# FFN-down with ten instead of nine of sixteen squares in seven-product form, the residual kept off chip between sweeps, and some weight sums moved into w_out

## The chip, the core and the metric

The kernel runs on one NeuronCore of a Trainium2 chip. TensorE (PE) multiplies, VectorE (DVE) and ScalarE (ACT) do the elementwise work, SyncE (SP) issues nearly all DMAs, in order, on one queue. The metric is the device time of one execution in microseconds (us).

## The reference

One decoder layer on 256 tokens of width 2048, in float32. Only the middle matters here:

```
x  = x + mix @ w_out                                   # 2048 x 2048
h2 = rms_norm(x, mlp_norm)
x  = x + square(relu(h2 @ w_ffn_up)) @ w_ffn_down      # 2048 x 8192, 8192 x 2048
gate = sigmoid(rms_norm(x, ple_norm) @ w_ple_gate)
x  = x + gate * (p @ w_ple_proj)
out = rms_norm(x, final_norm)
```

Ahead of it stand an input projection, a pooling mixer and an RWKV-7 time mixer, which the change does not touch.

## The kernel before, in words

Every matrix product is made from rounded parts: an operand a is split in a high part (a rounded copy, made by ScalarE) and a low part (a minus its high part, made by VectorE), and a product is three matmuls: high by high, low by high, high by low. So each weight that comes from DRAM passes through ScalarE and VectorE before PE can use it.

*Buffers.* Weights land in `raw` buffers, a ring of six [128, 1024] tiles (`RING`, L151; three in one pool, three in a later pool), and are split into rings of five `wh` (high) and four `wl` (low). A load waits on SP until its buffer is free, and what stands behind it on SP waits too. Big fixed buffers `a0` to `a5` ([128, 2048] each, `a8`) hold activations and the residual x, which is two tiles of 1 MiB, one for output columns 0 to 1023 (pair 0) and one for 1024 to 2047 (pair 1).

*w_out* (`gemm_toks`, from L1170): four chunks of 512 output columns, each of eight double rows of weights, 96 matmuls a chunk. After each chunk the new part of x is transposed into `h2`.

*FFN-up* (`gemm_wide`, L1121; matmuls L1135 and L1140) runs in two halves (`ffn_half`) of eight chunks f; each chunk has two groups of 16 k rows, and after each group `square` (L1410 to L1412) takes relu and square out of the wide PSUM bank. Each group gives one "pair" of activation rows, 16 per half. The chunks of the second half are f = 8 to 15.

*FFN-down* follows each half as two sweeps (`sweep`), one for each pair of output columns, with 16 "squares" each: a 2 by 2 block product of activations (two k tiles, two token tiles) by weights b11, b12, b21, b22 (two k tiles, two groups of 512 columns). A *plain* square makes the eight block products, 24 matmuls of 512 columns. A *seven-product* square uses a Strassen-like form: seven products, 21 matmuls. Three of them (p1, p2, p3) use the blocks b11, b21, b22 ("of_blocks"), four (p5, p7, p6, p4) use sums of blocks t1 to t4 ("of_sums"). p2, p3, p4 and d22 are PSUM banks shared with the plain squares; p1, p6, p5, p7 lie in two wide banks w1 and w2, and are combined by VectorE (the tile u, L1362 to L1365) after the last seven-product square. All matmuls of a sweep are recorded at one line, L1230; the tile in its name is d_p (banks p2, p3, p4), d_d (d22) or d_w (wide banks).

*Weights of a seven-product square* (`weights_seven`): w7h and w7l are the high and low parts of the blocks (L1281 to L1284), the four sums are made in place in the raw buffers (L1286 to L1289), and th and tl are their high and low parts (L1292, L1294). th and tl have one buffer each. For the squares in `AHEAD` the sums are made earlier, during FFN-up, by `sums_ahead` (VectorE L1219, L1223, L1224 from raw_ta into ta), stored to DRAM (L1226, tile tad) and loaded again in the sweep into buffer a4 (L1339, tile tr). One `sums_ahead` follows each FFN-up chunk. Before: `PLAIN` is 0, 3, 6, 9, 12, 14, 15, `AHEAD` is 2, 5, 8, 11, and the other seven-product squares are 1, 4, 7, 10, 13.

*Order in a seven-product square.* If the next square is also of seven products, the sums come first, else the blocks, so that th and tl of the next one can be written early. PE's order was written by hand only up to w_out; from there the scheduler orders every engine's instructions by priorities and its own estimate of when they are ready, and that order is fixed when the kernel is built.

*Residual.* x for the two pairs lies in buffers a3 and a4. The result of a sweep is scaled and added to it (`scaled_residual`, L1384): two wide ones after u, and four of 512 columns at the end of the last square. `x_store` (L1388) and `x_load` (L1391) move a tile of x to DRAM and back: pair 1 goes out after chunk 1, and at square 3 of the second sweep of each half the x of the other pair goes out and the one of this sweep comes into a3. In the last sweep pair 1 comes into a4 at square 12, with the load of p (`split_p`).

Of the kernel before, what the change touches and what calls it, by code (L numbers as in the profile page):

```python
# [40 lines left out]
def trunk(  # L41
# [62 lines left out]
    make_identity(nc, ident)  # L104
    ones = const.tile([128, 128], F32, name="ones")
    with tc.high_priority(40000):
# [1038 lines left out]
    def transposed(name):  # L1145
# [22 lines left out]
        return part, lambda k: hl[:, :, k, :]  # L1168

    h2_part, h2 = transposed("h2")  # L1170
# [33 lines left out]

    PLAIN = (0, 3, 6, 9, 12, 14, 15)
    AHEAD = (2, 5, 8, 11)
    SEVEN = tuple(i for i in range(16) if i not in PLAIN)
    dr = ctx.enter_context(tc.tile_pool(name="dr", bufs=1, space=bass.MemoryType.DRAM))
    saved = {}

    def sums_ahead(hf, np_, i):

        ra, rb = (
            load_raw(w_down[np_, hf * 16 + i, r].rearrange("p a n -> p (a n)"), 1024, f"ta{hf}{np_}_{i}_{r}") for r in range(2)
        )
        b11, b22, b12, b21 = ra[:, 0:512], ra[:, 512:1024], rb[:, 0:512], rb[:, 512:1024]
        t = fp.tile([128, 4, 512], F32, tag="th", name=f"ta{hf}{np_}_{i}")
        with tc.high_priority(20000):
            nc.vector.tensor_tensor(  # L1219
                t[:, 1:3], ra.rearrange("p (c n) -> p c n", c=2)[:, ::-1], b12.unsqueeze(1).to_broadcast([128, 2, 512]),  # L1220
                op=ALU.subtract,
            )
            nc.vector.tensor_tensor(t[:, 0], b11, t[:, 1], op=ALU.add)  # L1223
            nc.vector.tensor_tensor(t[:, 3], b21, t[:, 0], op=ALU.subtract)  # L1224
        d_ = saved[hf, np_, i] = dr.tile([128, 2, 1024], F32, tag=f"ta{hf}{np_}_{i}", name=f"tad{hf}{np_}_{i}")
        nc.sync.dma_start(d_.rearrange("p r n -> p (r n)"), t.rearrange("p c n -> p (c n)"))  # L1226
    F_A11, F_A12, F_A22, F_S2, F_S3, F_S4, F_S1 = range(7)
# [12 lines left out]
    def square_plain(src, pr):  # L1240

        q = PLAIN.index(pr)
        if pr == PLAIN[-1]:
            plains[:] = [fp.tile([128, 1024], F32R, tag="yd", name=f"yd{pr}")]
        elif q % 2 == 0:
            plains[:] = [a8((1, 2, 0)[q // 2], f"yd{pr}", F32R)]
        d = plains[0][:, q % 2 * 1024 : (q % 2 + 1) * 1024]
        split_sb(d[:, 0:512], d[:, 512:1024], src)

        def block(i, j):  # L1250
            o = j * T + i * 128
            return d[:, o : o + 128], d[:, 512 + o : 512 + o + 128]

        return block

    def square_seven(src, pr):

        if pr == SEVEN[-1]:
            y = a8(5, f"ys{pr}", F32R)[:, 0:1792]
        else:  # L1260
            y = fp.tile([128, 1792], F32R, tag="ys", bufs=NYS, name=f"ys{pr}")
# [41 lines left out]

    def sweep(src, acts, hf, np_, name, residual_, hooks=()):
# [22 lines left out]
        for i in range(npair):  # L1327
# [4 lines left out]
            if kept_sums is None:  # L1332
                rb, tr = load_raw(src[np_, i, 1].rearrange("p a n -> p (a n)"), 1024, f"{name}_1_{i}"), None
            else:
                rb = ring("raw", F32, f"raw_{name}_1_{i}")
                nc.sync.dma_start(rb[:, 512:1024], src[np_, i, 1, :, 1])
                tr = a8(4, f"tr_{name}_{i}").rearrange("p (r n) -> p r n", r=2)
                for r in range(2):
                    nc.sync.dma_start(tr[:, r], kept_sums[:, r])  # L1339
                tr = [tr[:, r] for r in range(2)]  # L1340
            if i in SEVEN:
# [44 lines left out]
    def x_store(np_):  # L1386
        xd[np_] = dr.tile([128, 2, 1024], F32, tag=f"xd{len(xd)}{np_}", name=f"xd{len(xd)}{np_}")
        nc.sync.dma_start(xd[np_], xc.pop(np_))  # L1388
# [4 lines left out]
    def split_p():  # L1393
# [4 lines left out]
        return t_[:, 0:512], t_[:, 512:1024]  # L1398

    xd, ps_ = {}, []  # L1400

    def ffn_half(hf):
        acts = []
        for i in range(8):
# [189 lines left out]
```

## Time and profile before

| | before |
|---|---|
| median of 3 runs | 1166.19 us (1165.98 to 1168.64) |
| profiled execution | 1166.29 us |
| its span, first to last instruction | 1164.2 us |
| busy: PE, VectorE, ScalarE | 1153.3, 903.5, 686.2 us |
| granted TensorE clock, mean | 0.999 |
| w_out chunks 1 to 3 with the transposes | about 303 to 371 us of the span |
| FFN-up half 0, then sweeps 1 and 2 | about 371 to 551, 551 to 632, 632 to 713 us |
| FFN-up half 1, then sweeps 3 and 4 | about 713 to 891, 891 to 972, 972 to 1053 us |
| DMA traffic | 269.36 MB |

How to read it: busy time is the time in which an engine has an instruction in work. PE's matmuls overlap and their ends are modelled, so PE's busy time also covers short waits; what a matmul costs is read from the distance of starts. The chain of waits is followed back from the last instruction: each piece was either released by the piece before it or came next on its engine. In a row with a bracket, the bracket gives the idle time of the engine just before the instruction and what ended it.

### The profile page before, as it was taken

The numbers are of one execution on the slowest core, as the hardware profiler recorded it, in microseconds if no ns is written. First come the engines' busy times: TensorE is split into PE (matmuls) and PEld (weight loads), VectorE is DVE, ScalarE is ACT, GpSimd is POOL, SyncE is SP. The second block draws the span as 40 slices with busy tenths as digits, with TensorE's granted clock in tenths as the row PEclk, the third lists the DMA queues.
The fourth block names the chain that finished last, engine by engine and source line by source line (L and its number), as shares of the span: only waits on it lengthen the run. The fifth ranks groups of instructions, "written<-read, shape, count | busy, mean of one in ns | idle before, by whom it ended". The sixth has DMA issues, their size and how long they took to land.

```text
span 1164.2 us, 19240 instructions
## 1 busy us (share of the span) xinstructions
PE 1153.3 (99%) x7360; PEld 991.6 (85%) x7360; DVE 903.5 (78%) x1193; ACT 686.2 (59%) x1216; POOL 17.2 (1%) x77
## 2 busy tenths in 40 slices
PE   9999999999999999999999999999999999999997
PEld 8999998788888888888888888888888888888886
DVE  7886898356555887887989988778878899898843
ACT  5868555667555555555665664555555664669733
POOL 4100000000000000000000000000000000000000
PEclk9999999999999999999999999999999999999999
DMA  7554444453766888787776867878987777876812
GB/s 274 164 172 129 157 155 148 146 164 109 254 190 212 298 313 285 257 305 263 250 265 236 300 234 240 313 273 286 320 291 234 265 270 260 289 285 223 301 55 73
DMA packets 73547, 269.36 MB, mean 231 GB/s; under 512 B 8176, under 2 KB 9200, under 8 KB 70512
## 3 DMA queue, kind: packets, MB, share of 16 engines
q1 hardware_dynamic: 73168, 267.78, 66.9%
q8 instruction: 57, 0.93, 0.3%
q10 hardware_dynamic: 288, 0.37, 0.1%
q14 instruction: 34, 0.28, 0.1%
HBM read 246.09 MB, written 22.02 MB: 230 GB/s over the span
## 4 chain that ended last, share of the span: by engine, by line
PE 97%; DVE 1%; ACT 1%; DMA 0%; issue 0%; ACTq 0%; DVEq 0%
PE u_w L1135 20%; PE d_p L1230 16%; PE u_w L1140 10%; PE d_w L1230 8%; PE d_d L1230 3%; PE o_b L193 2%; PE o_b L194 2%; PE o_b L195 2%; PE gt_b L193 2%; PE gt_b L195 2%; PE gt_b L194 2%; PE zp_b L193 1%; PE wag_b L380 1%; PE zr_b L184 1%; PE zk_b L184 1%; PE zk_b L185 1%
## 5 line engine op out<-in xcount | busy, mean ns | idle before, releaser
L1135 PE MATMUL u_w<-h,wh_u 128*128 128x512 f32 x1024 | 321.7, 395 | 0.0
L171 ACT ACTIVATE wh_u<-raw_u 128x512 fp32r<-128x512 f32 x256 | 147.5, 624 | 155.9 <-PE u_w L1135 107.7
L1140 PEld LDWEIGHTS u_w<-h,wl_u 128*128 128x128 f32 x1024 | 192.3, 188 | 45.3
L1140 PE MATMUL u_w<-h,wl_u 128*128 128x256 f32 x1024 | 201.5, 278 | 0.0
L172 DVE TENSOR_TENSOR wl_u<-raw_u,wh_u 128x1024 fp32r<-128x1024 f32 x128 | 156.2, 1221 | 47.3 <-PE u_w L1140 36.3
L1135 PEld LDWEIGHTS u_w<-h,wh_u 128*128 128x128 f32 x1024 | 156.0, 189 | 0.1
L1230 PE MATMUL d_p<-wh_d,yd 128*128 128x512 f32 x336 | 89.8, 389 | 0.0
L1230 PEld LDWEIGHTS d_p<-wh_d,yd 128*128 128x128 f32 x336 | 62.9, 188 | 13.0
L1292 ACT ACTIVATE th_d<-raw_d 128x1024 fp32r<-128x1024 f32 x40 | 40.4, 1052 | 55.7 <-DVE raw_d L1288 55.7
L171 ACT ACTIVATE wh_d<-raw_d 128x512 fp32r<-128x512 f32 x112 | 63.9, 621 | 9.0 <-ACT th_d L1292 4.1
L172 DVE TENSOR_TENSOR wl_o<-raw_o,wh_o 128x1024 fp32r<-128x1024 f32 x32 | 39.1, 1224 | 35.3 <-PE o_b L195 19.6
L172 DVE TENSOR_TENSOR wl_d<-raw_d,wh_d 128x1024 fp32r<-128x1024 f32 x56 | 66.1, 1219 | 0.6 <-PE u_w L1140 0.6
L171 ACT ACTIVATE wh_o<-raw_o 128x512 fp32r<-128x512 f32 x64 | 36.9, 625 | 36.8 <-issue 17.8
L1230 PE MATMUL d_w<-th_d,ys 128*128 128x512 f32 x216 | 55.1, 390 | 0.1
L1294 DVE TENSOR_TENSOR tl_d<-raw_d,th_d 128x1024 fp32r<-128x1024 f32 x40 | 47.4, 1222 | 7.7 <-ACT th_d L1292 7.7
L1230 PE MATMUL d_p<-wl_d,yd 128*128 128x512 f32 x168 | 51.7, 389 | 0.0
L1281 ACT ACTIVATE w7h_d<-raw_d 128x1024 fp32r<-128x1024 f32 x36 | 38.1, 1060 | 21.6 <-PE d_d L1230 11.2
L1294 DVE TENSOR_TENSOR tl_d<-tr_d,th_d 128x1024 fp32r<-128x1024 f32 x32 | 37.8, 1222 | 13.6 <-ACT th_d L1292 13.6
L1230 PEld LDWEIGHTS d_w<-th_d,ys 128*128 128x128 f32 x216 | 40.4, 188 | 9.1 <-ACT th_d L1292 0.8
L1283 DVE TENSOR_TENSOR w7l_d<-raw_d,w7h_d 128x1024 fp32r<-128x1024 f32 x36 | 43.9, 1220 | 3.1 <-PE u_w L1140 1.6
L1230 PE MATMUL d_p<-w7h_d,ys 128*128 128x512 f32 x144 | 44.3, 389 | 0.0
L1292 ACT ACTIVATE th_d<-tr_d 128x1024 fp32r<-128x1024 f32 x32 | 32.2, 1053 | 12.1 <-PE d_p L1230 12.0
(393 smaller groups left out, 2646.7 us busy)
## 6 DMA issues: line engine op xcount, KB each, us to landing
raw_u<-in_w_ffn_up_dram SPq DMA_DIRECT2D x128, 512.0 KB, 5.7
raw_d<-in_w_ffn_down_dram SPq DMA_DIRECT2D x112, 512.0 KB, 4.9
raw_o<-in_w_out_dram SPq DMA_DIRECT2D x32, 512.0 KB, 3.6
raw_ta<-in_w_ffn_down_dram SPq DMA_DIRECT2D x32, 512.0 KB, 4.3
tad<-ta SPq DMA_DIRECT2D x16, 1024.0 KB, 5.9
tr_d<-tad SPq DMA_DIRECT2D x32, 512.0 KB, 5.0
raw_gt<-in_w_ple_gate_dram SPq DMA_DIRECT2D x24, 512.0 KB, 4.6
raw_zk<-in_w_in_dram SPq DMA_DIRECT2D x16, 512.0 KB, 3.5
```

The lines of the kernel that those rows point to most:

```text
L171: nc.scalar.activation(wh[:, a * 512 : (a + 1) * 512], raw[:, a * 512 : (a + 1) * 512], AF.Copy)
L172: nc.vector.tensor_tensor(wl, raw, wh.bitcast(F32), op=ALU.subtract)
L193: nc.tensor.matmul(o, a_h, wh[:, 0:n], start=first, stop=False)
L194: nc.tensor.matmul(o, a_l, wh[:, 0:n], start=False, stop=False)
L195: nc.tensor.matmul(o, a_h, wl[:, 0:n], start=False, stop=last)
L1135: nc.tensor.matmul(bank[:, ct, :].rearrange("p (s t) -> p s t", s=2), wh[:, c], hl, start=k == 0, stop=False, skip_group_check=True,)
L1140: nc.tensor.matmul(bank[:, ct, 0:T], wl[:, c], hl[:, 0, :], start=False, stop=k == 15, skip_group_check=True)
L1230: nc.tensor.matmul(o, l, r, start=first, stop=last, skip_group_check=True)
L1281: nc.scalar.activation(ha, ra, AF.Copy)
L1283: nc.vector.tensor_tensor(la, ra, ha.bitcast(F32), op=ALU.subtract)
L1292: nc.scalar.activation(th[:, r], tr[r], AF.Copy)
L1294: nc.vector.tensor_tensor(tl[:, r], tr[r], th[:, r].bitcast(F32), op=ALU.subtract)
```

## The change

- `PLAIN` becomes 2, 5, 8, 11, 14, 15 and `AHEAD` 1, 4, 7, 10, 12. Squares 0, 3, 6, 9, 13 make their sums in place. A sweep starts with a seven-product square, and squares 12 and 13 are two in a row.
- Square 0 has an order of its own, and p5, p7 lie in w1, p1, p6 in w2 (before the other way round).
- Weight sums made ahead: one in each of w_out's chunks 1 to 3, before double row 4; one after each of the FFN-up chunks 0 to 6 of half 0; two after chunks 0 to 2 (f = 8 to 10) and one after chunks 3 to 6 of half 1; none after the eighth chunk of a half.
- x: both pairs go out after chunk 1; each sweep loads its pair into a4 at square 13; the second sweep of each half stores the pair of the first at square 3, and pair 1 goes out once more after f = 8. In the last sweep pair 1 comes into a3 at square 14. a3 holds the activations of square 4 meanwhile.
- As a4 holds x at a sweep's two ends, the sums of square 12, and of square 1 in a second sweep, are loaded into `raw` buffers.
- The `raw` ring has seven buffers; `ones` moves to a pool that ends earlier, and the `yd` tile of the last plain square goes.

```
-    RING = {"raw": (3, 3), "wh": (3, 2), "wl": (3, 1)}
+    RING = {"raw": (3, 4), "wh": (3, 2), "wl": (3, 1)}
...
+    PLAIN = (2, 5, 8, 11, 14, 15)
+    AHEAD = (1, 4, 7, 10, 12)
...
+    todo = [[((hf + j) % 2, i) for j in range(2) for i in AHEAD] for hf in range(2)]
+    def sums_next(hf, n):
+        for _ in range(n):
+            sums_ahead(hf, *todo[hf].pop(0))
...
-            run(gemm_toks(w_out[n], mix, f"o{n}", lambda banks: residual(banks, n)))
+            run(gemm_toks(w_out[n], mix, f"o{n}", lambda banks: residual(banks, n), None, {4: lambda: sums_next(0, 1)}))
...
-        p1, p6, p5, p7 = w1[:, 0], w1[:, 1], w2[:, 0], w2[:, 1]
+        p5, p7, p1, p6 = w1[:, 0], w1[:, 1], w2[:, 0], w2[:, 1]
...
-                tr = a8(4, f"tr_{name}_{i}").rearrange("p (r n) -> p r n", r=2)
+                if i == AHEAD[-1] or i == AHEAD[0] and not early:
+                    tr = [ring("raw", F32, f"raw_{name}_{r}_{i}") for r in (2, 3)]
+                else:
+                    tr = a8(4, f"tr_{name}_{i}")
+                    tr = [tr[:, 0:1024], tr[:, 1024:2048]]
...
-                for part in (of_sums, of_blocks) if i + 1 in SEVEN else (of_blocks, of_sums):
-                    part()
+                if i == 0:
+                    (s5, s7, s6, s4), (s1, s2_, s3) = sums_, blocks
+                    for step, (which, o, f, t) in (
+                        (put_high, s5), (put_high, s7), (put_high, s4), (put, s2_), (put_high, s6), (put_low, s5),
+                        (put_low, s7), (put_low, s4), (put_low, s6), (put, s3), (put, s1),
+                    ):
+                        step(which, o, a(f), w[t], False)
+                else:
+                    for part in (of_sums, of_blocks) if i + 1 in SEVEN else (of_blocks, of_sums):
+                        part()
...
             if f == 1:
                 inv_ms()
+                x_store(0)
                 x_store(1)
-            sums_ahead(hf, i // 4, AHEAD[i % 4])
+            if f == 8:
+                x_store(1)
+            sums_next(hf, (1 if hf == 0 or i > 2 else 2) if i < 7 else 0)
...
-            hooks = {3: lambda: (x_store(1 - np_), x_load(3, np_))} if j else {}
+            hooks = {13: lambda: x_load(4, np_)}
+            if j:
+                hooks[3] = lambda: x_store(1 - np_)
             if hf and j:
-                hooks[max(AHEAD) + 1] = lambda: (x_load(4, 1), ps_.extend(split_p()))
-            sweep(w_down[:, hf * 16 : hf * 16 + 16], acts, hf, np_, f"d{hf}{np_}", scaled_residual, hooks)
+                hooks[14] = lambda: (x_load(3, 1), ps_.extend(split_p()))
+            sweep(w_down[:, hf * 16 : hf * 16 + 16], acts, hf, np_, f"d{hf}{np_}", scaled_residual, hooks, j == 0)
```

More of the change, by code (lines that the diff above doesn't have):

```diff
@@ L104, in trunk @@
     make_identity(nc, ident)
-    ones = const.tile([128, 128], F32, name="ones")
+    ones = mc.tile([128, 128], F32, name="ones")
     with tc.high_priority(40000):
@@ L1168, in transposed, with sums_ahead @@
         return part, lambda k: hl[:, :, k, :]
+    PLAIN = (2, 5, 8, 11, 14, 15)
+    AHEAD = (1, 4, 7, 10, 12)
+    SEVEN = tuple(i for i in range(16) if i not in PLAIN)
+    dr = ctx.enter_context(tc.tile_pool(name="dr", bufs=1, space=bass.MemoryType.DRAM))
+    saved = {}
+    def sums_ahead(hf, np_, i):
+        ra, rb = (
+            load_raw(w_down[np_, hf * 16 + i, r].rearrange("p a n -> p (a n)"), 1024, f"ta{hf}{np_}_{i}_{r}") for r in range(2)
+        )
+        b11, b22, b12, b21 = ra[:, 0:512], ra[:, 512:1024], rb[:, 0:512], rb[:, 512:1024]
+        t = fp.tile([128, 4, 512], F32, tag="th", name=f"ta{hf}{np_}_{i}")
+        with tc.high_priority(20000):
+            nc.vector.tensor_tensor(
+                t[:, 1:3], ra.rearrange("p (c n) -> p c n", c=2)[:, ::-1], b12.unsqueeze(1).to_broadcast([128, 2, 512]),
+                op=ALU.subtract,
+            )
+            nc.vector.tensor_tensor(t[:, 0], b11, t[:, 1], op=ALU.add)
+            nc.vector.tensor_tensor(t[:, 3], b21, t[:, 0], op=ALU.subtract)
+        d_ = saved[hf, np_, i] = dr.tile([128, 2, 1024], F32, tag=f"ta{hf}{np_}_{i}", name=f"tad{hf}{np_}_{i}")
+        nc.sync.dma_start(d_.rearrange("p r n -> p (r n)"), t.rearrange("p c n -> p (c n)"))
+    xd, ps_, nst = {}, [], [0]
+    todo = [[((hf + j) % 2, i) for j in range(2) for i in AHEAD] for hf in range(2)]
+    def sums_next(hf, n):
+        for _ in range(n):
+            sums_ahead(hf, *todo[hf].pop(0))
     h2_part, h2 = transposed("h2")
@@ L1203, in keep @@
             split_sb(wh, wl, raw[:, a * 512 : (a + 1) * 512])
[L1205 to L1226, printed above, removed]
     F_A11, F_A12, F_A22, F_S2, F_S3, F_S4, F_S1 = range(7)
@@ L1256, in square_seven @@
     def square_seven(src, pr):
-        if pr == SEVEN[-1]:
-            y = a8(5, f"ys{pr}", F32R)[:, 0:1792]
+        if pr in (4, SEVEN[-1]):
+            y = a8(3 if pr == 4 else 5, f"ys{pr}", F32R)[:, 0:1792]
         else:
@@ L1302, in weights_seven, with sweep @@
         }
-    def sweep(src, acts, hf, np_, name, residual_, hooks=()):
+    def sweep(src, acts, hf, np_, name, residual_, hooks=(), early=False):
         hooks = dict(hooks)
@@ L1336, in sweep @@
                 nc.sync.dma_start(rb[:, 512:1024], src[np_, i, 1, :, 1])
-                tr = a8(4, f"tr_{name}_{i}").rearrange("p (r n) -> p r n", r=2)
+                if i == AHEAD[-1] or i == AHEAD[0] and not early:
[3 more added lines that the diff above has]
+                    tr = [tr[:, 0:1024], tr[:, 1024:2048]]
                 for r in range(2):
-                    nc.sync.dma_start(tr[:, r], kept_sums[:, r])
-                tr = [tr[:, r] for r in range(2)]
+                    nc.sync.dma_start(tr[r], kept_sums[:, r])
             if i in SEVEN:
@@ L1386, in x_store @@
     def x_store(np_):
-        xd[np_] = dr.tile([128, 2, 1024], F32, tag=f"xd{len(xd)}{np_}", name=f"xd{len(xd)}{np_}")
+        nst[0] += 1
+        xd[np_] = dr.tile([128, 2, 1024], F32, tag=f"xd{nst[0]}", name=f"xd{nst[0]}")
         nc.sync.dma_start(xd[np_], xc.pop(np_))
@@ L1398, in split_p @@
         return t_[:, 0:512], t_[:, 512:1024]
-    xd, ps_ = {}, []
     def ffn_half(hf):
```

4 lines of the change are left out of this document (1 added, 3 removed).

## The prediction, on record before the change was run

> **What bounds the kernel now.** I read the page first (span, and the chain that ended last), then the busy times by stage, then the chain in order of time at the ends of the four FFN-down sweeps, and last VectorE's instructions at one such end.
>
> ```profile
> span 1164.2 us, 19240 instructions
> ...
> PE 97%; DVE 1%; ACT 1%; DMA 0%; issue 0%; ACTq 0%; DVEq 0%
> ```
>
> The chain that sets the end is TensorE (PE) for 97% of the span. The stages that the change touches, by busy time (columns: PE, weight load, DVE, ACT, POOL, each in us with its count; then clock, DMA share, GB/s):
>
> ```profile
> 551.00:632.00 81.00, 81.00 (x359) 67.07 (x358) 73.01 (x79) 49.59 (x68) 0.00 (x0) 1.00 0.71 242
> 632.00:713.00 81.00, 80.95 (x357) 66.68 (x356) 73.61 (x79) 48.03 (x67) 0.00 (x0) 1.00 0.74 262
> 713.00:891.00 178.00, 178.00 (x1023) 155.27 (x1023) 141.72 (x191) 93.53 (x175) 0.00 (x0) 1.00 0.83 289
> 891.00:973.00 82.00, 82.00 (x364) 67.95 (x363) 73.73 (x81) 50.40 (x68) 0.00 (x0) 1.00 0.70 244
> 973.00:1054.00 81.00, 81.00 (x358) 66.82 (x357) 75.02 (x83) 50.44 (x71) 0.00 (x0) 1.00 0.81 288
> ```
>
> Rows 1, 2, 4 and 5 are the sweeps, row 3 is the second half of FFN-up. PE is never idle in them, so PE work taken out is time taken out, as long as VectorE, 73 to 75 us busy of 81, keeps up. That is the second thing to watch: a sweep has two engines near their limit, and VectorE makes what PE eats.
>
> How much of the 81 us is matmuls and how much is hidden waiting, the chain in order of time tells (start, length, what, how many instructions). The first row starts sweep 1, the second sweep 2, the third ends sweep 2, the fourth starts sweep 4, the last ends it:
>
> ```profile
> 550.73 4.09 PE d_p L1230 x18
> ...
> 631.66 4.08 PE d_p L1230 x18
> ...
> 711.63 1.36 PE d_d L1230 x6
> ...
> 972.26 4.08 PE d_p L1230 x18
> ...
> 1052.04 1.36 PE d_d L1230 x6
> ```
>
> A sweep has 7 plain squares of 24 matmuls and 9 seven-product squares of 21, together 357. A matmul takes 4.08 / 18 = 0.2267 us. 357 of them are 80.93 us. Sweep 1 takes 631.66 - 550.73 = 80.93: no loss. Sweep 2 takes 711.63 + 1.36 - 631.66 = 81.33: 0.40 lost. Sweep 4 takes 1052.04 + 1.36 - 972.26 = 81.14: 0.21 lost. The loss of sweep 2 lies at its second square, where th (the rounded weight sums) comes late:
>
> ```profile
> 637.10 0.47 PE d_p L1230 x2
> ...
> 637.59 0.65 ACT th_d L1292
> 638.24 0.04 issue
> 638.28 1.65 PE d_w L1230 x6
> ```
>
> The code of that square puts the products of sums (d_w) ahead of the block products (d_p); here block products run first. So PE's order is the scheduler's, which lets what is ready go first.
>
> **The change part by part.** *One square more in seven products.* A sweep becomes 6 x 24 + 10 x 21 = 354 matmuls, 3 fewer. Four sweeps: 12 x 0.2267 = 2.72 us off the path. With the 0.40 + 0.21 us of present loss this is all that the four sweeps can give back: 3.33 us, 0.29% of the time.
>
> *VectorE per sweep.* The start and end of sweeps decide the rest; this is VectorE across the end of sweep 1 (at 631.66 sweep 2 starts), and then ScalarE's two th of the second square:
>
> ```profile
> 624.15 2.48 DVE L1384 SCALAR_TENSOR_TENSOR x<-u_d,s2sq,x 128x1024 f32<-128x1024 f32 x2
> 626.55 1.22 DVE L172 TENSOR_TENSOR wl_d<-raw_d,wh_d 128x1024 fp32r<-128x1024 f32 x1
> 627.69 0.75 DVE L1384 SCALAR_TENSOR_TENSOR x<-d_p,s2sq,x 128x512 f32<-128x512 f32 x1
> 628.35 1.22 DVE L172 TENSOR_TENSOR wl_d<-raw_d,wh_d 128x1024 fp32r<-128x1024 f32 x1
> 629.48 1.61 DVE L1384 SCALAR_TENSOR_TENSOR x<-d_p,s2sq,x 128x512 f32<-128x512 f32 x2
> 631.53 0.69 DVE L1284 TENSOR_TENSOR w7l_d<-raw_d,w7h_d 128x512 fp32r<-128x512 f32 x1 [0.44 <-PE d_d L1230]
> 632.13 0.74 DVE L1384 SCALAR_TENSOR_TENSOR x<-d_d,s2sq,x 128x512 f32<-128x512 f32 x1
> 632.80 1.22 DVE L1283 TENSOR_TENSOR w7l_d<-raw_d,w7h_d 128x1024 fp32r<-128x1024 f32 x1
> 634.04 0.69 DVE L1286 TENSOR_TENSOR raw_d<-raw_d,raw_d 128x512 f32<-128x512 f32 x1
> 634.77 0.69 DVE L1287 TENSOR_TENSOR raw_d<-raw_d,raw_d 128x512 f32<-128x512 f32 x1
> 635.50 0.69 DVE L1288 TENSOR_TENSOR raw_d<-raw_d 128x512 f32<-128x512 f32 x1
> 636.22 0.69 DVE L1289 TENSOR_TENSOR raw_d<-raw_d,raw_d 128x512 f32<-128x512 f32 x1
> 636.97 1.23 DVE L1283 TENSOR_TENSOR w7l_d<-raw_d,w7h_d 128x1024 fp32r<-128x1024 f32 x1
> 638.11 2.35 DVE L1294 TENSOR_TENSOR tl_d<-raw_d,th_d 128x1024 fp32r<-128x1024 f32 x2
> ```
>
> ```profile
> 636.22 2.01 ACT L1292 ACTIVATE th_d<-raw_d 128x1024 fp32r<-128x1024 f32 x2 [3.85 <-DVE raw_d L1288]
> ```
>
> Taken from start to start (ends overlap a little), a wide subtraction costs 1.14 us (626.55 to 627.69), a half one 0.60 (631.53 to 632.13), a sum 0.73, a residual about 0.66. A plain square needs two wide ones, 2.28. A square whose sums were made ahead needs w7l 1.14 + 0.60 and tl 2.35, 4.1. One whose sums are made in place needs 2.9 more, 7.0. Before, a sweep has 7, 4 and 5 of these, after 6, 5 and 5: 1.8 us more. So VectorE has 73.0 + 1.8 = 74.8 to 75.0 + 1.8 = 76.8 of 354 x 0.2267 = 80.25 us. It stays below PE over a whole sweep, with 3 to 5 us of slack instead of 6 to 8. I take 0 for the middle of a sweep, where three squares repeat unchanged (7.0 + 4.1 + 2.3 = 13.4 of VectorE on 66 x 0.2267 = 14.96 of PE).
>
> *The start of the second sweep of each half* is where I expect to pay. Before, its first square was plain. Now it is a square with sums made in place. Its w7l needs two of the ring's four wl buffers, and these come free only when PE is through the last square but one of the old sweep; in the rows above that buffer is written at 626.55, right behind two residuals. From 626.55: 1.14 + 0.60 + four sums 2.93, and three or four residuals of 0.66 that come between (the higher priority), gives 633.2 to 633.9 for the fourth sum. The second th is one ACT instruction of 1.0 us behind it: 634.2 to 634.9. PE is free for the square at 631.66. If it takes the nine block products first (2.04 us, until 633.70), it waits 0.5 to 1.2 us; if it keeps the new order, which puts a product of the second th first, 2.5 to 3.2 us. A gain is bounded too: the present loss of that place goes, since the square that now loses is replaced. Bounds 0.1 to 3.2 per start; I take 0.8, since the trace shows block products run ahead when th is late. Two starts: +1.6, less the 0.61 of now: +1.0.
>
> *The start of the first sweep of each half* follows FFN-up, where the wl ring turns over every 16 matmuls and w7l of the first square can be written several us ahead, and the sums_ahead that sat at the end of FFN-up is gone (none for the eighth chunk). p5 and p7 move to the wide bank freed first; p1 and p6 wait for VectorE's last square, behind 9 matmuls that need neither. 0, up to 1.0 each.
>
> *The end of every sweep.* Squares 12 and 13 now both have seven products; before, 12 was plain. w7l of 13 must wait for the two wl of plain square 11, so VectorE idles and then has w7l 1.7, sums 2.9, tl 2.35 and the four wl of 14 and 15 to make, with the u sums and two residuals between. I get the last wl at about 16.9 us after square 12's start, wanted at 16.1 (2 x 4.76 + 5.44 + five matmuls); the 16 products of square 15 with high weights can go first. 0, up to 0.8 each.
>
> *x off chip.* x goes out after use and comes back into slot 4 at square 13, ahead of square 13's weights on SP's queue. Two loads and two stores of 1 MiB more. The load waits for tl of square 10, some 10 us ahead of need; behind it wait the weights of 13, whose own buffers come free only about then. In the second sweep the store at square 3 replaces a store and a load. 0 on the path; cover gone, one landing of some us at a sweep's end.
>
> *Weight sums.* Four more chunks: one each inside w_out 1 to 3, seven in FFN-up half 0, ten in half 1, two each in its first three chunks. A chunk is VectorE 1.2 + 0.7 + 0.7 (the wide and half rows above) and 1.05 MB in and 1.05 MB out.
>
> ```profile
> 318.00:350.00 32.00, 32.00 (x147) 26.09 (x147) 18.16 (x20) 15.85 (x30) 0.00 (x0) 1.00 0.61 191
> ```
>
> In w_out VectorE is busy 18.16 of 32 us and DMA 0.61: 2.6 us and 2.1 MB per 96 matmuls (21.8 us, 96 GB/s, 0.31 more) fit. 0, up to 0.7 per chunk.
>
> ```profile
> 824.00:847.00 23.00, 23.00 (x133) 20.07 (x133) 17.94 (x24) 12.16 (x23) 0.00 (x0) 1.00 0.91 323
> ```
>
> ```profile
> SPq L163 <- DVE wl_u L172: 118.9, 56, 3.9
> ```
>
> In FFN-up 323 GB/s at a share of 0.91 is 355 GB/s when full. Chunks 8 to 10 now want 3 x (4.19 + 4.19) MB, 1.05 for the store of x and 1.05 for an early reload of sums, 27.3 MB: 76.8 us at 355 against 3 x 22.25 = 66.75 of PE. That is 10 us short. Against it stands a ring of seven buffers and SP's row: over half 1 SP waited 118.9 us for VectorE to free a buffer, so loads run far ahead of PE (a w_up buffer is 2.8 us of PE work, four in the wl ring and five or so in the raw ring, some 20 us). Bounds 0 to 10; I take 0.
>
> The Trainium skill ("DMA: Bandwidth & Descriptors", Measured) has a core alone reach 425 GB/s in large transfers. By that, 27.3 MB take 64 us and nothing is short; no row quoted here goes beyond 323, so it only speaks against the flood below.
>
> Sum against the profiled execution (1166.29 us: the span and 2.1 us around it; 0.1 above the median of 1166.19): 1166.3 - 2.7 + 1.0 = **1164.6**.
>
> **The rivals.** *Clean* (0.24): the second starts cost nothing, for instance because block products and a quick th cover it; 1166.3 - 3.3 = 1163.0. For it: sweep 1's start loses nothing now. Against: the 5.1 us between 626.55 and 631.66 hold 4.7 of work and three residuals.
>
> *VectorE late, PE in the written order* (0.14): 3.2 us at both second starts in place of the present 0.61: 1166.3 - 2.7 + 6.4 - 0.6 = 1169.4. For it: VectorE at 95%, and the new order puts the second th first. Against: the block products at 637.10 that ran ahead of the written order.
>
> *Slower: the DMA flood at FFN-up 8 to 10* (0.13). If queue order lets the two pairs of sums sit ahead of w_up loads and the ring runs dry, PE waits there for what is not covered of 10 us. It decides from 5.1 us uncovered (1164.6 + 5.1 = 1169.7, the 0.3% bound); with one raw buffer's worth (2.8) covered, 7.2: 1171.8. For it: 0.91 in the rows already. Against: SP's 118.9 us.
>
> **How the numbers follow.** The forecast has 0.49. About 0.3% (3.5 us) is what a measurement of this kernel can tell from no change, and it lies just beyond the 3.33 us that the sweeps hold; so faster takes the clean case and scatter or a small gain elsewhere: 0.12. Slower is the flood and the upper part of the late VectorE: 0.17. Same: 0.71. Range 1162.6 (clean, with 0.4 of scatter) to 1169.5 (late VectorE): it leaves out some 0.05 below and 0.15 above.
>
> **What would show it.** Right: 1416 matmuls on L1230's line, sweeps 1 and 3 at 80.3 us, sweeps 2 and 4 at about 81, with th of the first square the last release there; FFN-up still 178.3 us per half. Wrong: a PE gap in chunks 8 to 10 behind w_up loads (flood), gaps at square 15 (ends), or a second sweep of over 83 us.

## The result, and the profile after

The changed kernel takes 1180.7 us (median of 4 runs, 1179.73 to 1181.44), the kernel before 1166.3 in the same runs (median of 4): ratio 1.0119, 95% interval 1.0101 to 1.0136. It is 14 us slower, where 1164.6 was forecast and the range ended at 1169.5. The profiled execution took 1179.73 us. Its page begins:

```profile
span 1178.0 us, 19307 instructions
...
PE 89%; DVE 6%; DMA 2%; issue 1%; ACT 1%; SPq 0%; DVEq 0%; ACTq 0%
```

The chain that ended last went through PE for 97% of the span before; now 89%, and VectorE has 6%. PE still reads as 98% busy (1156.4 us) on this page: the loss is not seen in the shares of busy time. It is seen in the busy times by stage (PE, weight load, DVE, ACT, POOL with counts; then clock, DMA share, GB/s):

```profile
552.00:632.00 80.00, 80.00 (x354) 65.91 (x353) 70.98 (x77) 47.83 (x66) 0.00 (x0) 1.00 0.75 259
632.00:718.00 86.00, 81.86 (x354) 66.89 (x353) 75.02 (x81) 49.35 (x69) 0.00 (x0) 0.98 0.75 269
718.00:899.00 181.00, 179.26 (x1028) 156.06 (x1027) 151.45 (x209) 95.36 (x178) 0.00 (x0) 1.00 0.86 313
899.00:980.00 81.00, 81.00 (x358) 66.76 (x357) 72.16 (x78) 48.50 (x66) 0.00 (x0) 1.00 0.73 256
980.00:1066.00 86.00, 81.86 (x351) 66.42 (x350) 74.84 (x81) 51.23 (x71) 0.00 (x0) 0.98 0.80 285
```

Sweeps 1 and 3 (rows 1 and 4) are as forecast: PE never idle, 354 matmuls in 80 to 81 us. Rows 2 and 5, the second sweep of each half, each have 4.1 us in which PE has nothing, and the clock is below 1.00. Row 3, FFN-up's second half, has 1.7 idle. From the start of the first matmul of each stage in the two traces:

| us | before | after | difference |
|---|---|---|---|
| until FFN-up half 0 | 371.33 | 372.17 | +0.84 |
| FFN-up half 0 | 179.24 | 179.45 | +0.21 |
| sweeps 1 and 2 | 162.26 | 167.05 | +4.79 |
| FFN-up half 1 | 178.34 | 180.35 | +2.01 |
| sweeps 3 and 4 | 162.06 | 167.59 | +5.53 |
| the rest | 110.97 | 111.39 | +0.42 |

One sweep of 354 matmuls at 0.2267 us would be 80.25. The four take 80.54 (551.62 to 632.16), 86.51, 80.56 and 87.03: nearly all of the loss is in the second of each half. What PE waited for, in total, how often and at most:

```profile
PE d_w L1237 <- ACT th_d L1297: 4.8, 2, 2.4
PE d_p L1237 <- DVE w7l_d L1288: 3.5, 2, 1.7
PE u_w L1140 <- DVE wl_u L172: 1.7, 1, 1.7
```

One wait of each of the first two kinds in each second sweep, and one wait in FFN-up. Here is PE at the start of sweep 2 (632.16); the bracket is the idle time before the instruction and what ended it:

```profile
632.84 0.61 PE L1237 MATMUL d_p<-w7h_d,ys 128*128 128x512 f32 x2
635.21 0.51 PE L1237 MATMUL d_p<-w7l_d,ys 128*128 128x512 f32 x1 [1.75 <-DVE w7l_d L1288]
638.10 2.07 PE L1237 MATMUL d_w<-th_d,ys 128*128 128x512 f32 x4 [2.39 <-ACT th_d L1297]
639.97 1.05 PE L1237 MATMUL d_p<-th_d,ys 128*128 128x512 f32 x2
...
647.76 1.07 PE L1237 MATMUL d_p<-wh_d,yd 128*128 128x512 f32 x4
```

PE does five matmuls of block products, waits 1.75, does one more, waits 2.39, and then its matmuls come at 0.47 us each (638.10 to 639.97 for four). The one between the waits, and the two at 632.84 ahead of it, are a block product of square 1: the scheduler put it into square 0, ahead of the products of sums, and its last matmul waits for square 1's w7l (square 0's own w7l was written from 629.02 on). From 632.16 to 647.76 there are two squares, 42 matmuls, 9.52 us of work in 15.60: 6.1 lost. Why th and that w7l are late stands in VectorE's instructions across the sweep's end:

```profile
611.79 0.69 DVE L1289 TENSOR_TENSOR w7l_d<-raw_d,w7h_d 128x512 fp32r<-128x512 f32 x1 [1.61 <-PE d_d L1237]
...
619.85 3.49 DVE L172 TENSOR_TENSOR wl_d<-raw_d,wh_d 128x1024 fp32r<-128x1024 f32 x3
623.26 0.68 DVE L1379 TENSOR_TENSOR u_d<-d_w,u_d 128x512 f32<-128x512 f32 x1
...
629.02 1.22 DVE L1288 TENSOR_TENSOR w7l_d<-raw_d,w7h_d 128x1024 fp32r<-128x1024 f32 x1
...
633.33 0.68 DVE L1292 TENSOR_TENSOR raw_d<-raw_d,raw_d 128x512 f32<-128x512 f32 x1
633.93 1.22 DVE L1288 TENSOR_TENSOR w7l_d<-raw_d,w7h_d 128x1024 fp32r<-128x1024 f32 x1
635.07 0.69 DVE L1293 TENSOR_TENSOR raw_d<-raw_d 128x512 f32<-128x512 f32 x1
635.67 0.69 DVE L1289 TENSOR_TENSOR w7l_d<-raw_d,w7h_d 128x512 fp32r<-128x512 f32 x1
636.27 0.69 DVE L1294 TENSOR_TENSOR raw_d<-raw_d,raw_d 128x512 f32<-128x512 f32 x1
```

Square 13's w7l (first row) waits for PE to leave plain square 11. Behind it everything is late: three wl run ahead of u, and square 0's w7l starts at 629.02, 3.1 us before PE reaches the square, where the trace of before had 5.1 for the wl in that place. Square 1's w7l (633.93 and 635.67) then stands between square 0's sums, and the fourth sum starts at 636.27, 4.1 us after PE began. Last, the clock in that stretch:

```profile
632.00:638.00 6.00, 1.96 (x8) 1.06 (x6) 6.00 (x9) 3.20 (x5) 0.00 (x0) 0.97 0.63 226
638.00:641.00 3.00, 2.90 (x7) 2.32 (x8) 1.30 (x2) 0.05 (x1) 0.00 (x0) 0.50 0.79 249
641.00:648.00 7.00, 7.00 (x33) 5.78 (x32) 5.43 (x5) 5.47 (x7) 0.00 (x0) 1.00 0.90 292
```

PE is busy 1.96 of 6 us, and the next 3 us are granted half a clock. From 638.10 to 641.64 nine matmuls take 3.54 us instead of 2.04: 1.5 us. So 1.75 + 2.39 + 1.5 = 5.6 of the 6.1; PE's modelled ends hide the rest, since from start to start the two waits add 1.9 and 2.7 to a matmul's 0.23. Sweep 4 repeats it to the hundredth: waits of 1.75 and 2.39 at 982.62 and 985.51.

FFN-up's gap, early in the fourth chunk of half 1, behind the last of the three doubles; first on VectorE, then on PE:

```profile
785.88 1.23 DVE L1184 TENSOR_TENSOR ta<-raw_ta,raw_ta 128x1024 f32<-128x1024 f32 x1 [1.21 <-DMA tad<-ta]
...
789.43 1.22 DVE L172 TENSOR_TENSOR wl_u<-raw_u,wh_u 128x1024 fp32r<-128x1024 f32 x1
```

```profile
790.70 0.50 PE L1140 MATMUL u_w<-h,wl_u 128*128 128x256 f32 x2 [1.74 <-DVE wl_u L172]
```

The second of two weight sums in a row waits until the first one's store has left their one buffer, and the wl that PE wants stands behind it on VectorE.

### The profile page after: what moved, and what is told of

Its sections match the earlier page's. It is cut to its first block, busy times and chain, and to the rows that moved or that the text cites. A ratio compares the mean times of both kernels' runs of the same rounds, so it can differ in the third digit from the quotient of the medians.

```text
span 1178.0 us, 19307 instructions
## 1 busy us (share of the span) xinstructions
PE 1156.4 (98%) x7348; PEld 990.4 (84%) x7348; DVE 921.1 (78%) x1225; ACT 689.6 (59%) x1220; POOL 18.3 (2%) x77
## 4 chain that ended last, share of the span: by engine, by line
PE 89%; DVE 6%; DMA 2%; issue 1%; ACT 1%; SPq 0%; DVEq 0%; ACTq 0%
PE u_w L1135 19%; PE d_p L1237 13%; PE u_w L1140 10%; PE d_w L1237 9%; PE d_d L1237 2%; PE o_b L193 2%; PE o_b L194 2%; PE o_b L195 2%; PE gt_b L195 2%; PE gt_b L193 2%; PE gt_b L194 2%; PE zp_b L193 1%; PE zr_b L184 1%; PE zk_b L184 1%; PE zk_b L185 1%
## 5 line engine op out<-in xcount | busy, mean ns | idle before, releaser
L1297 ACT ACTIVATE th_d<-raw_d 128x1024 fp32r<-128x1024 f32 x52 | 52.4, 1051 | 65.3 <-DVE raw_d L1293 65.0
L1237 PE MATMUL d_p<-wh_d,yd 128*128 128x512 f32 x288 | 77.0, 389 | 0.0
L1299 DVE TENSOR_TENSOR tl_d<-raw_d,th_d 128x1024 fp32r<-128x1024 f32 x52 | 61.5, 1222 | 12.2 <-ACT th_d L1297 11.6
L1237 PE MATMUL d_w<-th_d,ys 128*128 128x512 f32 x240 | 63.9, 400 | 4.8 <-ACT th_d L1297 4.8
L171 ACT ACTIVATE wh_d<-raw_d 128x512 fp32r<-128x512 f32 x96 | 54.7, 619 | 17.9 <-PE d_p L1237 7.7
L1237 PEld LDWEIGHTS d_p<-wh_d,yd 128*128 128x128 f32 x288 | 54.1, 188 | 11.2
L172 DVE TENSOR_TENSOR wl_d<-raw_d,wh_d 128x1024 fp32r<-128x1024 f32 x48 | 56.8, 1218 | 5.3 <-PE d_p L1237 5.3
L1237 PE MATMUL d_p<-w7h_d,ys 128*128 128x512 f32 x160 | 49.8, 393 | 0.0
L1237 PE MATMUL d_p<-wl_d,yd 128*128 128x512 f32 x144 | 44.3, 389 | 0.0
L172 DVE TENSOR_TENSOR wl_zp<-raw_zp,wh_zp 128x1024 fp32r<-128x1024 f32 x16 | 19.4, 1220 | 24.6 <-ACT wh_zp L171 24.6
```

Source lines behind the costliest of these rows:

```text
L171: nc.scalar.activation(wh[:, a * 512 : (a + 1) * 512], raw[:, a * 512 : (a + 1) * 512], AF.Copy)
L172: nc.vector.tensor_tensor(wl, raw, wh.bitcast(F32), op=ALU.subtract)
L1237: nc.tensor.matmul(o, l, r, start=first, stop=last, skip_group_check=True)
L1297: nc.scalar.activation(th[:, r], tr[r], AF.Copy)
L1299: nc.vector.tensor_tensor(tl[:, r], tr[r], th[:, r].bitcast(F32), op=ALU.subtract)
```

## The experiments

Two theories stood against each other for the second sweeps: VectorE comes late (V), or loads come late behind the reload of x and of sums (D); and two for FFN-up: the one buffer of the sums (B), or too many bytes at once (F).

**e1_plain_first.** The second sweeps begin with a plain square again, and each seven-product square with sums in place is followed by one with sums ahead; all else is as after.

```
+    SEQ = (tuple(range(16)), (2, 0, 1, 5, 3, 4, 8, 6, 7, 11, 9, 10, 14, 13, 12, 15))
-        for i in range(npair):
+        for pos, i in enumerate(seq):
```

> Second sweeps of each half take their squares in the order 2, 0, 1, 5, 3, 4, 8, 6, 7, 11, 9, 10, 14, 13, 12, 15: a plain square first, then sums in place, then sums made ahead. First sweeps and everything else as in the changed kernel. Theory V (VectorE cannot finish the sums and the high and low parts of a sums-in-place square by the time PE asks for it first): each second sweep loses at most 0.5 us of its 80.25, as before the change, and the time falls by some 12 us to 1168 to 1170. Rival D (the loads are late: x traffic and four more raw buffers at the start of a second sweep): the loss of about 6 us per second sweep stays, time 1177 to 1181. Rival E (the lateness of VectorE at the end of the first sweep is enough by itself): 2 to 3 us per second sweep stay, 1172 to 1175.

Measured 1174.0 us (1173.56 to 1175.46), ratio 1.0069 (1.0053 to 1.0086). Sweeps 1 and 2 take 163.06 instead of 167.05, 3 and 4 165.56 instead of 167.59. The waits:

```profile
PE pp_b L193 <- DVE xb L1401: 2.7, 1, 2.7
...
PE d_w L1238 <- ACT th_d L1298: 0.7, 2, 0.4
```

The wait for th falls from 4.8 to 0.7, and a new one of 2.7 stands at the end of sweep 4: only one plain square now follows the last sums, so the residuals are late. V holds for the first square of a second sweep, where PE no longer waits. The sum is not V's but the one that rival E gave (2 to 3 us kept per second sweep, 1172 to 1175): sweeps 1 and 2 keep 2.6 us over 160.5, most of it from 647 to 655, behind a weight load that lands at 646.42 and the sums that follow. e5 below takes 1.8 of these 2.6 away by the end of the first sweep alone.

**e3_sums0_ahead.** In the second sweeps square 0 has its sums made ahead and square 1 makes them in place: VectorE's four sums leave the critical place, while the loads remain.

```
+    AHEAD1 = (0, 4, 7, 10, 12)
-    todo = [[((hf + j) % 2, i) for j in range(2) for i in AHEAD] for hf in range(2)]
+    todo = [[((hf + j) % 2, i) for j in range(2) for i in (AHEAD, AHEAD1)[j]] for hf in range(2)]
```

> In second sweeps square 0 has its sums made ahead and square 1 makes them in place (the other way round in the changed kernel); the order of squares stays 0, 1, 2. Loads at the start are as many as before. Theory V: th of square 0 needs no sums any more, VectorE has 2.9 us less ahead of it, so square 0 loses under 1.5 us, square 1 some 1 to 2; a second sweep loses 1.5 to 3.5 instead of 6.4, and no pause reaches 2.4 us. Rival D: the sums of square 0 come through raw buffers as those of square 1 did, the loss stays 5 to 7. Time 1172 to 1175 by V, 1179 to 1182 by D.

Measured 1175.10 us (one run; before 1166.37 on the same chip); sweeps 163.36 and 165.68. The first 9 us of sweep 2, and the waits:

```profile
632.00:638.00 6.00, 6.00 (x28) 4.93 (x27) 6.00 (x8) 3.09 (x6) 0.00 (x0) 1.00 0.91 300
638.00:641.00 3.00, 3.00 (x15) 2.49 (x14) 3.00 (x4) 1.44 (x2) 0.00 (x0) 1.00 0.99 394
```

```profile
PE d_w L1238 <- ACT th_d L1298: 1.9, 4, 0.7
...
PE d_p L1238 <- ACT wh_d L171: 1.5, 1, 1.5
```

PE is busy throughout at full clock, beside more traffic than in after (300 and 394 GB/s against 226 and 249). So at the start of the sweep it is the four sums that PE lacked, and not the loads (D falls there). Late loads aren't without a share, though: the 1.5 us for wh, at 996 in sweep 4, go back to a weight load,

```profile
988.37 6.99 DMA raw_d<-in_w_ffn_down_dram
```

and the clock falls behind it, so that sweep 4 loses nearly 5 us, more than the 3.5 that V allowed.

**e4_end_swap.** The first sweep of each half ends with squares 13, 12, 14, 15, so that 13, with sums in place, isn't kept waiting behind 12; the second sweeps are as in after.

```
+    SEQ = (tuple(range(12)) + (13, 12, 14, 15), tuple(range(16)))
```

> First sweeps end 13, 12, 14, 15 instead of 12, 13, 14, 15 (sums in place ahead of sums made ahead, as in the rest of a sweep); second sweeps still begin with square 0. It prices one term: VectorE's lateness at the end of the first sweep. If the 2 us by which w7l of the next square 0 starts late (3.1 us ahead of PE instead of 5.1) is worth its length, second sweeps lose about 4 us or less instead of 6.4, time 1175 to 1177; if the order of the sums alone decides, 6 stay and the time is 1180.

Measured 1175.69 us (one run); sweeps 163.99 and 165.64, 3.1 and 2.0 us less than after. VectorE and PE's waits:

```profile
626.38 1.22 DVE L1289 TENSOR_TENSOR w7l_d<-raw_d,w7h_d 128x1024 fp32r<-128x1024 f32 x1
...
633.93 0.68 DVE L1295 TENSOR_TENSOR raw_d<-raw_d,raw_d 128x512 f32<-128x512 f32 x1
```

```profile
PE d_p L1238 <- DVE w7l_d L1289: 2.9, 2, 1.4
PE d_w L1238 <- ACT th_d L1298: 2.4, 2, 1.2
```

Square 0's w7l starts 2.6 us earlier than in after, the fourth sum 2.3, and PE reaches the square 0.8 earlier (631.33). The two waits are down to 1.4 and 1.2 us in both second sweeps, 1.5 less in sum. The clock does not follow the waits alone; these are stretches of 3.41 us, two in sweep 2 and two in sweep 4:

```profile
634.04:637.46 3.42, 2.21 (x8) 1.61 (x9) 3.42 (x4) 1.06 (x1) 0.00 (x0) 1.00 1.00 350
637.46:640.87 3.41, 3.41 (x16) 2.82 (x15) 2.44 (x4) 2.29 (x3) 0.00 (x0) 1.00 0.92 302
...
978.79:982.20 3.41, 1.02 (x3) 0.66 (x4) 3.41 (x5) 2.11 (x2) 0.00 (x0) 1.00 0.93 330
982.20:985.62 3.42, 3.42 (x9) 2.66 (x9) 1.32 (x3) 0.00 (x0) 0.00 (x0) 0.50 0.91 321
```

In sweep 2 it stays at 1.00 and in sweep 4, with the same waits, it falls to 0.50. So the waits price VectorE's lateness at the end of the first sweep at 1.5 us a half. Sweeps 1 and 2 gain 3.1 because the clock was spared as well, sweeps 3 and 4 only 2.0.

**e12_sums_first.** The four sums and two th of the second sweep's first square get a higher priority; PE's order is unchanged.

```
-                w = weights_seven(ra, rb, tr, f"{name}_{i}")
+                w = weights_seven(ra, rb, tr, f"{name}_{i}", 12000 if i == 0 and not early else 0)
...
+            with tc.high_priority(up):
                 if tr is None:
```

> The kernel after with one thing more: the four sums and the two th of the second sweep's first square get a higher priority, so that on VectorE they stand ahead of that square's second w7l and of one of the two w7l of square 1; TensorE's order is the same. If VectorE's order at that place is a part of the cause, the fourth sum ends 0.6 to 1.2 us earlier, the two waits of each second sweep (1.75 and 2.39 us) shrink by as much, and if the clock then stays at 1.00, as it did when the waits were 1.44 and 1.19, another 1.4 us go: sweeps 1 and 2 take 164.4 to 166.4 us instead of 167.05, sweeps 3 and 4 as much less. If PE's wait is for square 1's block product (its w7l, which now comes later), the first wait grows by as much as the second shrinks and the sum stays at 167.

Measured 1180.47 us (one run; before 1166.72); sweeps 167.42 and 168.05, no better than after. PE's waits, and the clock:

```profile
PE d_p L1237 <- DVE w7l_d L1287: 4.7, 2, 2.4
PE d_w L1237 <- ACT th_d L1297: 2.4, 2, 1.2
```

```profile
638.00:641.00 3.00, 3.00 (x8) 2.32 (x8) 1.33 (x2) 0.00 (x0) 0.00 (x0) 0.50 0.73 277
641.00:644.00 3.00, 3.00 (x10) 2.35 (x10) 1.30 (x2) 1.94 (x3) 0.00 (x0) 0.65 0.85 270
```

The wait for th halves, and the wait for square 1's w7l, which is now made later, grows instead: the second theory. The sum of the two falls by 0.6 us at each place (2.35 + 1.16 in sweep 2), but the clock is half for 6.83 us at both places (3.41 in after), which takes that back. That this comes of the change isn't shown: e7, with the waits of after, has 6.83 us of it in sweep 2 as well. PE's place for square 1's product makes both waits count, one after the other; a kernel with that product behind the sums wasn't run.

**e2_two_buffers.** Two weight sums in a row use different buffers (and the sum in w_out's chunk 1 goes to FFN-up chunk 3).

```
-        t = fp.tile([128, 4, 512], F32, tag="th", name=f"ta{hf}{np_}_{i}")
+        t = fp.tile([128, 4, 512], F32, tag=("th", "tl")[len(saved) % 2], name=f"ta{hf}{np_}_{i}")
```

> Sums made ahead go alternately into the buffers th and tl (one buffer before), and the one of w_out's chunk 1 moves to FFN-up chunk 3 of half 0, as a second one there. Theory B (the second sum of a pair waits for the first one's store, since both use one buffer, and VectorE stands behind it): FFN-up half 1 goes from 180.35 to 178.4 us. Rival F (DMA flood: 355 GB/s is not enough for two sums per chunk): it stays at 180 or more. For w_out, if the late load of the sums in chunk 1 holds VectorE ahead of the residual: the first FFN-up matmul moves from 372.4 to about 371.6 us; if not, it stays. Second sweeps unchanged, each 6 us over. Time 1177 to 1179 on a run where the changed kernel has 1180.5.

Measured 1184.54 us (one run; before 1166.37): slower, and FFN-up half 1 takes 183.76 instead of 180.35. The chain there, a new wait, and the DMA engines in the 7 us ahead of the chain's first line:

```profile
784.38 0.33 SPq L1191
...
784.80 5.86 DMA raw_u<-in_w_ffn_up_dram
```

```profile
PE u_w L1135 <- ACT wh_u L171: 2.4, 1, 2.4
```

```profile
774.00:781.00 7.00, 7.00 (x43) 6.11 (x42) 6.16 (x10) 3.41 (x7) 0.00 (x0) 1.00 0.55 218
```

The wait for the buffer is gone, but a w_up load stands on SP behind the sums' store (L1191) and goes out at 784.80. It is late and not slow: its 5.86 us are below the median of this run's w_up loads, 6.2. SP had issued none since 774, as the two stores waited 7.2 and 2.9 us for VectorE, and the DMA engines were busy at a share of 0.55 meanwhile. B falls: what PE lacks is weights that queue behind the sums' stores. Of the 3.4 us more than in after, about 1.5 are half clock behind that wait (792.81 to 796.23).

**e7_spread.** The same ten sums, but the doubles after chunks f = 8, 11 and 14 and not after 8, 9 and 10.

```
-            sums_next(hf, (1 if hf == 0 or i > 2 else 2) if i < 7 else 0)
+            sums_next(hf, (2 if hf and i % 3 == 0 else 1) if i < 7 else 0)
```

> The changed kernel with only the double chunks of weight sums spread: 8, 11, 14 instead of 8, 9, 10. Theory F (three double chunks in a row want more than the DMA engines and SP's one queue give; the second buffer did not help): FFN-up half 1 goes from 180.35 to 178.4 to 179 us. Rival: a double chunk costs by itself, wherever it stands, and 180 to 181 stay. Sweeps unchanged (167 each two). Time 1178 to 1180.

Measured 1180.57 us (one run; before 1166.33), FFN-up half 1 178.33, as before the change (178.34); the sweeps are no better (167.62 and 169.55; sweep 4 has a third wait for th, of 1.8 us, behind the late load of p). A stretch of FFN-up half 1 in after, and then in this run:

```profile
741.00:763.00 22.00, 22.00 (x128) 19.18 (x127) 20.12 (x27) 12.14 (x24) 0.00 (x0) 1.00 0.97 361
```

```profile
741.00:763.00 22.00, 22.00 (x128) 19.16 (x127) 19.09 (x26) 13.26 (x25) 0.00 (x0) 1.00 0.91 334
```

Spread, the traffic is 334 GB/s and PE has no gap; bunched, it reached 361 at a share of 0.97 and PE ran dry at 789. Not the total but doubles in a row cost the 2.0 us, as F had it. That the DMA engines' rate sets this isn't shown: in after, too, SP issued no w_up load from 772.70 to 781.30, behind a sums' store that waited for VectorE, and from 774 to 781 the engines moved 310 GB/s at a share of 0.76.

**e8_x_alone.** The kernel before with x off chip alone: its squares, its sums and its ring of six buffers, and the new x_load and x_store.

```
+                x_store(0)
                 x_store(1)
...
-            hooks = {3: lambda: (x_store(1 - np_), x_load(3, np_))} if j else {}
+            hooks = {13: lambda: x_load(4, np_)}
+            if j:
+                hooks[3] = lambda: x_store(1 - np_)
```

> The kernel before, with nine squares in seven products in their old places, and x alone changed: both pairs out after chunk 1, in again at square 13 into a4, out at square 3 of second sweeps, once more after chunk 8; the sums of square 2 in a second sweep through raw buffers; ring of six. Theory V: x traffic costs little, 0 to 1 us in all, time 1166 to 1167.5, sweeps 162 to 162.7. Rival D: x traffic and the four raw buffers at a second sweep's start are what costs, 3 us or more per two sweeps, time 1172 or more.

Measured 1168.98 us (one run; before 1166.33, highest 1168.14); sweeps 163.01 and 162.63, 0.75 and 0.57 more than before. The stage after sweep 4 has 1.4 more as well (112.38). That lies between the two theories, and one profile doesn't tell all of it from scatter. Read as it stands, x costs the sweeps 1.3 us, where after lost 10.3; what x costs where VectorE is late it doesn't tell.

**e5_both_orders, e9_last_sasa, e10_last_saa, e11_none_in_wout.** These join what helped: the first sweeps of e4, the second of e1, the sums of e7. e9 and e10 change the last sweep's order, to leave two plain squares at its end; e11 is e9 without weight sums in w_out.

```
 e5   +    SEQ = (tuple(range(12)) + (13, 12, 14, 15), (2, 0, 1, 5, 3, 4, 8, 6, 7, 11, 9, 10, 14, 13, 12, 15))
 e9   +    last sweep: (2, 0, 1, 5, 3, 4, 8, 6, 7, 11, 9, 10, 13, 12, 14, 15)
 e10  +    last sweep: (2, 0, 1, 5, 3, 4, 8, 6, 7, 10, 11, 9, 12, 13, 14, 15)
 e11  -    {4: lambda: sums_next(0, 1)}                 # in w_out
      +    sums_next(hf, (2 if i % 3 == 0 else 1) if i < 7 else 0)
```

> All three repairs of order at once, on the changed kernel: first sweeps end 13, 12, 14, 15; second sweeps run 2, 0, 1, 5, 3, 4, 8, 6, 7, 11, 9, 10, 14, 13, 12, 15; the double chunks of weight sums in FFN-up half 1 are 8, 11 and 14 instead of 8, 9 and 10. If VectorE's lateness has the two parts measured so far (square 0 first, and the end of the first sweep), sweeps 1 and 2 take 161 to 162 us, sweeps 3 and 4 162 to 164 (the end with one plain square after the last sums cost 2.7 in the last sweep), FFN-up half 1 178.4 to 179.5, time 1165 to 1168. If late loads (rival D) set a floor behind VectorE, sweeps 1 and 2 stay near 163 and the time is 1169 to 1172.

> As the kernel with both orders and the spread double chunks, and only the last sweep's order changed so that two plain squares follow its last sums again: 2, 0, 1, 5, 3, 4, 8, 6, 7, 11, 9, 10, 13, 12, 14, 15. The 3.1 us by which the next product waited for the residual, and the half clock after it (1.9 us in the stage behind), should both go: sweeps 3 and 4 from 164.90 to 161 to 162.5 us, the stage behind from 112.9 to 111, time 1164.5 to 1166.5. If four seven-product squares in a row (9, 10, 13, 12) are more than VectorE can follow, 1 to 3 us come back inside the sweep: 1166 to 1169.

> The same with another order of the last sweep: 2, 0, 1, 5, 3, 4, 8, 6, 7, 10, 11, 9, 12, 13, 14, 15, that is at most three seven-product squares in a row. Same gain expected at the end, 1164.5 to 1166.5; sums in place right ahead of the two plain squares (13) may make u and the residual late as at the first sweeps' ends of the changed kernel, which costs nothing if only the next stage's first product waits under 1 us.

> e9_last_sasa with one thing more: no weight sums inside w_out, and both halves of FFN-up make ten, two after every third chunk. If the sums in w_out cost the 0.8 us that the first profile after showed at a chunk's end, FFN-up starts at 371.3 of the span, half 0 takes 178.4 to 179.3 as half 1 does with the same spread, and the median falls by 0.8 to 1.5 us below e9_last_sasa, to about 1166. If w_out's start of 372.2 was scatter of that run (two other kernels with the same sums started FFN-up at 371.3), the median stays at 1167 to 1168; if the three more sums in half 0 cost what they make PE wait for, half 0 is over 180 and the median above 1168. In neither case is it faster than the kernel before by over 0.3%.

| | median us | before | ratio, 95% interval | sweeps 1+2 | FFN-up half 1 | sweeps 3+4 |
|---|---|---|---|---|---|---|
| e5 | 1170.18 | 1166.33 | 1.0027 (1.0015 to 1.0039) | 161.29 | 178.34 | 164.90 |
| e9 | 1167.42 | 1166.55 | 1.0010 (1.0000 to 1.0019) | 161.63 | 178.33 | 162.85 |
| e10 | 1168.68 | 1166.55 | 1.0018 (1.0008 to 1.0028) | 161.31 | 178.34 | 164.01 |
| e11 | 1166.97 | 1166.47 | 1.0003 (0.9994 to 1.0012) | 161.26 | 178.34 | 163.06 |

Sweeps 1 and 2 show both causes apart and together: 167.05 in after, 163.06 with the new order of second sweeps (e1), 163.99 with the new end of first ones (e4), 161.29 with both (e5). The times of e5, e9 and e10 are above what was forecast first (1165 to 1168 for e5, 1164.5 to 1166.5 for the other two).

e5 keeps e1's wait at the end of sweep 4, and the clock falls there too:

```profile
PE pp_b L193 <- DVE xb L1401: 3.1, 1, 3.1
```

```profile
1056.30:1060.00 3.70, 3.61 (x9) 2.89 (x10) 3.70 (x6) 1.36 (x3) 0.00 (x0) 0.56 0.31 117
```

e9 takes that away: sweeps 3 and 4 fall from 164.90 to 162.85. e11 differs from it by less than the two intervals can tell, so the price of the sums in w_out stays open between nothing and some 2 us; FFN-up starts at 371.81 in e9 and at 371.64 in e11. None is faster than the kernel before: in e11 the four sweeps take 161.26 + 163.06 = 324.32 us, the same as before the change (162.26 + 162.06), with 12 matmuls less. 3.3 us above 321.0 remain; 1.3 of it are two waits for th, and the longer one goes back to p; the second row is VectorE:

```profile
PE d_w L1238 <- ACT th_d L1298: 1.3, 2, 0.9
```

```profile
1031.13 0.69 DVE L177 TENSOR_TENSOR ps<-raw_pT,ps 128x512 fp32r<-128x512 f32 x1 [0.69 <-ACT ps L176]
```

From start to start, 3.0 of the 3.3 us stand ahead of products of sums, 2.4 of them in sweeps 3 and 4. The largest, 1.2 at 1034, is the wait of 0.9: the split of p stands on VectorE between the sums (the row above) and waits for the load of p, which lands at 1030.44. So a part of what is left belongs to the order of other work on VectorE and not to the squares; no run moves that alone.

## Why the prediction was wrong, point by point

- **Twelve matmuls, -2.72 us**: right in kind: 1416 matmuls run, and sweeps 1 and 3 take 80.54 and 80.56, forecast 80.25, sweep 1 before 80.93.
- **The middle and the start of first sweeps, 0**: right within 0.3 each, by the same numbers.
- **The end of every sweep, 0**: right for PE and wrong for VectorE. PE ended the sweep on time, but VectorE was 2.5 us later than before (629.02 against 626.55), 2.0 of it against PE, and the next term was worked out as if it were not.
- **The start of the second sweep, 0.8 each, bounds 0.1 to 3.2**: this is the step that failed. Measured 6.1 by the end of the second square. It took 626.55 from the trace of before as the time when square 0's w7l is written, although the term ahead of it had just made VectorE's work there longer. From that w7l it allowed 6.65 to 7.35 us to the end of the fourth sum; it was 7.9 (629.02 to 636.88), because square 1's w7l, 1.7 us, stood between the sums. It let PE choose between nine block products and the written order; PE had a third order, fixed when the kernel was built: one block product of square 0, one of square 1 whose last weights come late, and then the sums. And it had no term for the clock, 1.5 us in sweep 2 of the profiled run. e4 takes 1.5 us of waiting off each half by VectorE's earlier start alone, e1 and e3 some 4 us off the first half by taking the sums off that place, and e5, with both orders, leaves 0.8 of the first half's 6.5.
- **The rival "VectorE late, PE in the written order"** named the right engine, place and cause, with a chance of 0.14, and at 3.2 us a start half the price. PE's order wasn't the written one, and the clock isn't in it either.
- **Weight sums in FFN-up, 0, bounds 0 to 10**: 2.0. The sum of bytes wasn't what decided, since the same bytes spread cost nothing (e7), nor was SP's long wait for buffers a cover. What the traces show at the gaps is the order of two queues: a sum that waits for its buffer with a wl behind it on VectorE, and w_up loads behind a sums' store on SP (e2, and after as well). The prediction reckoned bytes against time and named no instruction that waits. No run kept the doubles in a row and changed SP's order alone.
- **The Trainium skill's 425 GB/s** ("DMA: Bandwidth & Descriptors", Measured) was taken to speak against the flood. The traces come near it over a few microseconds: 422 GB/s from 786 to 789 in FFN-up of after, and 416 from 791 to 797 in e2. Over 22 us at a share of 0.97 it was 361, near the 355 that the prediction worked out as full from the row of before. So 355 is no bound here.
- **x off chip, 0**: 1.3 us in the sweeps by one profile of e8; open. **w_out, 0**: FFN-up started 0.84 later in the profile of after, but with the same sums it started anywhere from 371.28 (e7) to 373.25 (e10), before the change at 371.33; open, and small.

The sum: of the +13.8 us of the span the four sweeps have +10.3 (forecast -2.7 + 1.0), FFN-up's second half +2.0 (forecast 0) and the other stages +1.5 (forecast 0).

## What to carry to other kernels

When an engine that feeds PE has only a few per cent of slack over a stage, don't ask whether it keeps up on average; walk its instructions across each boundary of the changed schedule, and take no start time there from the old trace once an earlier term has moved it. Where engines run in an order fixed at build time, a late piece is not passed over: list what stands behind it, on PE, on VectorE and on the DMA queue. A gain of 0.2% in PE work is less than one such pause.

## What the runs showed of the hardware

Short pauses can cost more than their length, and whether they do is in part luck. In these traces the granted clock is whole or half, and it turns only on steps of 3.41 us: between 330 and 1085 us of the span, 13 half stretches in seven runs last 3.41 us or 6.83, and the two in after start 348.16 us apart, 102 steps of 3.413. The steps lie differently in every execution. Where PE was busy for 1.65 us or less of a step at full clock, the next step was at half clock in all cases but one (1.62, e1); from 1.67 on it stayed at full.

So a pause costs its clock or not by how it falls on the steps. The same waits lost it in sweep 4 of e4 and not in sweep 2. FFN-up's single wait cost none in after (1.74 us, PE busy 1.67 of the step) and a half step in e4 (1.76, busy 1.65): FFN-up half 1 took 180.35 in the one and 181.94 in the other, 1.6 us apart, near the 1.7 that half of 3.41 gives.

The Trainium skill ("TensorE: Matmul & The Clock Gate", Part 1) has the clock fall to half after an idle window of about 3.4 us that runs freely, and rise after a busy one. The traces agree on the length, 3.41 us, and on its running freely. The window need not be idle, though: up to 1.65 us of work in it did not save the clock, and no single pause here that cost it was as long as 3.4 us.
